# Attention value steps one unit further behind their scores, traced ahead of the scores of the unit that takes their buffer

## The chip, the core and the metric

The kernel runs on one core of one Trainium2 chip. The core has five engines that run side by side, each through its own list of instructions in order: TensorE (PE, matrix products; PEld is its weight load), VectorE (DVE), ScalarE (ACT), GpSimd (POOL) and SyncE (SP). SP computes nothing here: nearly all DMA transfers are issued from its queue, one behind the other. The metric is the device time of one execution in microseconds (us), lower is better.

## What is computed

Two layers of a decoder on 1024 tokens of width 1024. Layer 0 uses mixer A (dilated sliding-window attention), layer 1 mixer B (sliding-window attention with sinks). Each is followed by a layer norm and a gate. Cut to what matters:

```python
def mixer_a(x, w_in, w_out, cos, sin):
    h = x @ w_in
    for gi, (window, dil) in enumerate(((128, 1), (512, 4), (2048, 16))):
        q, k, v = ...                       # 16 heads of 64, rope on q and k
        o, lse = banded_attention(strided(q), strided(k), strided(v), window // dil)
        ...
    wts = softmax(stack(lses))              # the three groups are merged
    o = einsum('gbsh,gbshd->bshd', wts, stack(outs))
    return (o * silu(z)) @ w_out

def banded_attention(q, k, v, max_dist, sinks=None):
    s = einsum(q, k) * dh ** -0.5           # scores in a band of keys
    e = exp(s - max(s))
    return einsum(e, v) / sum(e), lse

x = layer_norm(ALPHA * x + h); x = x + sigmoid(x @ w_gate) * (p @ w_proj)
```

## The kernel before

**Linear work.** Products in full precision are made of three half-precision ones: each operand is split into a high and a low part, and `lin` (L264 on) issues L270, L271 and L272 for each of 8 slices of the contraction. So one tile of 128 tokens by 512 columns is 24 matmuls, called linear matmuls below. Mixer A has 6 times a block of `v` tiles and two blocks of `q`/`k` tiles (8 tiles each), then `z` tiles; mixer B has fewer. Weights come in blocks: loaded (L102), their largest value found (L108 on DVE), split (L131 on ACT, L132 on DVE) while earlier blocks are multiplied.

**Units.** The attention is cut into units of four heads and one tile of 128 queries, against one or two tiles of keys: 96 units in mixer A, 32 in mixer B, numbered from 0. A unit has two steps. `score` computes the scores on PE (L383, 8 or 16 matmuls into `s`), adds the mask and takes the maximum (L387, DVE), makes the bias `nbias` (L391, ACT, written into the unit's `st`), the exponentials (L393, ACT), splits them into `phl` (L397 ACT, L399 POOL or DVE), and has the DMA transpose `phl` into `pT` (L402, SP). `value` multiplies `pT` with the values (L414 to L416, 12 or 24 matmuls into one half of `o`), copies the result into `st` (L694, ACT) and stores `st` to a scratch in DRAM (L703, SP). In mixer B the result goes through `mu` (L858, DVE) instead. The units of a `q`/`k` tile start about 1.67 tiles after it, since `rope_out` has to rotate, split and transpose the tile into `qk` (L345 to L360).

**Order around the change.** `sub_tick` is called after every third of a linear tile and adds `upt` thirds of credit; a full credit calls `unit_step`. This takes the next unit from the queue, pushes it into `self.pipe`, a list of `lag` entries, and takes the oldest one out. So the value step of a unit is traced `lag` unit steps after its scores: 2 in mixer A, 3 in mixer B. `upt` is 0.75 in most of mixer A, so units come every 1.33 tiles. The tracing order is not the last word: the program is then put in order for each engine by a scheduler that goes by a timeline of its own, and may put an instruction behind later ones when its operands come late there.

**Buffers.** A tile name with `bufs=n` has n buffers that are taken in turn; whoever takes one waits for the last reader of its previous content. `pT` has `lag + 1` (3 in mixer A, 4 in mixer B), the scratch row `st` of mixer A `lag + 2` = 4. So the scores of unit u + 4 write the `st` that unit u stored.

**Merges.** When the last of three groups of a token tile has its value, `merge` (L745 to L767) loads the three `st` rows back as `gt`, weighs and adds them (DVE, POOL) and stores the sum to `oa`. In `mixed`, behind mixer A, these rows are loaded (L894), multiplied with the gate, split, transposed and multiplied with the output weights.

Of the kernel before, what the change touches and what calls it, by code (L numbers as in the profile page):

```python
# [10 lines left out]
F32 = mybir.dt.float32  # L11
F16 = mybir.dt.float16
# [8 lines left out]
P = 128  # L21
# [5 lines left out]
HD = 64  # L27
# [111 lines left out]
class Trunk:  # L139
# [160 lines left out]
    def unit_step(self):  # L300

        if not (self.units or any(self.pipe)):
            return
        new = self.units.pop(0) if self.units else None
        old = self.pipe.pop()
        self.pipe.insert(0, new)
        if new:
            new["score"]()
        if old:
            old["value"]()  # L310

    def set_lag(self, lag):
        assert not any(self.pipe)
# [56 lines left out]
    def scores(self, qa, kas, mask, cs, ncs, sums, nbias, floor, pool_lo):  # L370

        nc, at = self.nc, self.att
        nb = len(kas)
        nk = nb * P
        sm = at.tile([P, 4, 2 * P], F32, tag="sm", name="sm", bufs=self.bufs)
        mx = self.small.tile([P, 4], F32, tag="mx", name="mx", bufs=6)
        for pr in range(2):
            ps = self.ps_s.tile([P, 2, 2 * P], F32, tag="s", name="s")
            for i in range(2):
                h = 2 * pr + i  # L380
                for kb, ka in enumerate(kas):
                    for sw in range(2):
                        nc.tensor.matmul(ps[:, i, kb * P:(kb + 1) * P], qa(h), ka(h, sw), start=(sw == 0),  # L383
                                         stop=(sw == 1))
            for i in range(2):
                h = 2 * pr + i
                nc.vector.tensor_tensor_reduce(sm[:, h, :nk], ps[:, i, :nk], mask, 1.0, -3e38, ALU.add, ALU.max,  # L387
                                               mx[:, h:h + 1])
        if floor is not None:
            nc.vector.tensor_max(mx, mx, floor)  # L390
        nc.scalar.activation(nbias, mx, AF.Copy, scale=ncs, bias=LN_PSCALE)  # L391
        for h in range(4):
            nc.scalar.activation(sm[:, h, :nk], sm[:, h, :nk], AF.Exp, bias=nbias[:, h:h + 1], scale=cs,  # L393
                                 accum_out=sums[:, h:h + 1])
        pf = at.tile([P, 16 * P], F16, tag="phl", name="phl", bufs=self.bufs)
        hl = pf[:, :8 * nk].rearrange("p (a h c) -> p a h c", a=2, h=4)
        nc.scalar.activation(hl[:, 0], sm[:, :, :nk], AF.Copy)  # L397
        eng = nc.gpsimd if pool_lo else nc.vector
        eng.tensor_sub(hl[:, 1], sm[:, :, :nk], hl[:, 0])  # L399
        pt = at.tile([P, 2, 4, 2, P], F16, tag="pT", name="pT", bufs=len(self.pipe) + 1)  # L400
        ptf = pt.rearrange("p a h b c -> p (a h b) c")[:, :8 * nb, :]
        nc.sync.dma_start(ptf, pf[:, :8 * nk], transpose=True)  # L402
        return ptf.rearrange("p (a h b) c -> p a h b c", a=2, h=4)
# [218 lines left out]
    def layer_a(self):  # L622
        nc, tc, a = self.nc, self.tc, self.a
        at = self.att
        self.o_dr = [self.dram.tile([P, D], F32, name=f"oa{n}", tag=f"oa{n}") for n in range(NT)]
        self.z_dr = [self.dram.tile([P, D], F32, name=f"za{n}", tag=f"za{n}") for n in range(NT)]
        scr = [[self.dram.tile([S, 2, 4 * HD + 8], F32, name=f"scr{g}_{i}", tag=f"scr{g}_{i}") for g in range(3)]
               for i in range(2)]

        self.x2_scale()  # L630
        self.set_lag(2)
        self.upt = 0.75
        vh = at.tile([P, 3, NT, 4 * HD], F16, tag="vh", name="vh", bufs=1)
        vl = at.tile([P, 3, NT, 4 * HD], F16, tag="vl", name="vl", bufs=1)
        slots = [2, 2]
        cvs = {}
        for pair in range(2):
            for g in (1, 2, 0):
                self.rope_tables(g)
                blk = self.next_block()  # L640
                cvs[pair, g] = self.prod(self.invx, blk.inv, 2.0 ** V_SHIFT, "cv")
                slots = [i for i in range(3) if i != slots[1]]
                pick = slice(slots[0], slots[1] + 1, slots[1] - slots[0])
                for n in range(NT):
                    ps = self.ps_lin.tile([P, 512], F32, tag="lin", name="lin")
                    self.lin(ps, blk, *self.stat_a(g, n), 0, 512)
                    self.v_out(ps.rearrange("p (s c) -> p s c", s=2), vh[:, pick, n, :], vl[:, pick, n, :])
                    self.progress()
                blk.released = True
                for i in range(2):  # L650
                    if pair and g == 0 and i:
                        self.upt = 1.0
                    blk = self.next_block()
                    cs, ncs = self.qk_scales(blk, self.invx)
                    v1, v2 = (v[:, slots[i]].rearrange("p n (h c) -> p n h c", c=HD) for v in (vh, vl))
                    qk = []
                    for n in range(NT):
                        ps = self.ps_lin.tile([P, 512], F32, tag="lin", name="lin")
                        self.lin(ps, blk, *self.stat_a(g, n), 0, 512)
                        qk.append(at.tile([P, 12, P], F16, tag="qk", name="qk", bufs=8))  # L660
                        self.rope_out(ps, 4, 4, n, qk[n])
                        self.unit_a(2 * pair + i, g, n, qk, v1, v2, cs, ncs,
                                    cvs[pair, g], scr)
                        self.progress()
                    blk.released = True
        self.merge_every = 1
        self.z_block(self.invx, lambda n: self.stat_a(0, n))
        self.drain()
# [15 lines left out]
    def unit_a(self, q, g, n, qk, vh, vl, cs, ncs, cv, scr):  # L684
        nc, at = self.nc, self.att
        tiles = [n] if g == 2 or (n % 2 == 0 if g == 1 else n == 0) else [n - 1, n]
        mask = self.mask_2 if g == 2 else self.mask_a[:, (2 - len(tiles)) * P:]

        def stats():
            st = at.tile([P, 4 * HD + 8], F32, tag="st", name="st", bufs=len(self.pipe) + 2)  # L690
            return st, st[:, 4 * HD:4 * HD + 4], st[:, 4 * HD + 4:]

        def outp(o, st):
            nc.scalar.activation(st[:, 0:4 * HD], o.rearrange("p h c -> p (h c)"), AF.Copy, scale=cv)  # L694
            d = scr[q // 2][g][:, q % 2, :]
            if g == 1:
                b = 512 * (n % 2) + n // 2
                d = d[b:b + 509:4]
            elif g == 2:
                d = d[n:n + 1017:8]  # L700
            else:
                d = d[n * P:(n + 1) * P]
            nc.sync.dma_start(d, st)  # L703
            if g == 0 and q % 2:
                self.merges.append(self.merge(n, q // 2, scr[q // 2]))

        kas = [lambda h, sw, t=qk[i]: t[:, 4 + 4 * sw + h, :] for i in tiles]
        self.later(UNIT_LAG, lambda: self.unit(lambda h: qk[n][:, h, :], kas, mask, cs, ncs,
                                          lambda h, kb: vh[:, tiles[kb], h, :], lambda h, kb: vl[:, tiles[kb], h, :],
                                          stats, outp, n % 4 != 0))  # L710
# [76 lines left out]
    def layer_b(self, xT, invx):  # L787
        nc, at = self.nc, self.att
        self.o_dr = [self.dram.tile([P, D], F32, name=f"ob{n}", tag=f"ob{n}") for n in range(NT)]
        self.z_dr = [self.dram.tile([P, D], F32, name=f"zb{n}", tag=f"zb{n}") for n in range(NT)]  # L790
        self.set_lag(3)
        self.bufs = 3
        self.rope_tables(0)
        self.sk_cs = self.kv.tile([P, 16], F32, name="sk_cs", tag="sk_cs")
# [349 lines left out]
```

## Time and profile before

| | us |
|---|---|
| median of 3 runs (lowest) | 1680.08 (1678.07) |
| the profiled execution, its own time | 1672.76 |
| its span, first to last instruction | 1670.9 |
| PE busy | 1587.2 |
| DVE busy | 1080.0 |
| ACT busy | 922.0 |
| POOL busy | 671.6 |

The profile is one execution. Mixer A lies between 80 and 1000 us of its span, the output and gate of layer 0 up to 1250, mixer B from 1250 to 1480, the rest is output and gate of layer 1. A row of a waits view says which instruction of which engine stood idle, and whose end it was released by, with the sum, the number of times and the longest. A row of a timeline has the start, the length, the engine, line and operation, what it writes and reads, and, in brackets, the idle time before it. In a row of SP's queue the length is the time the issue of that transfer held the queue, not the transfer itself.

### The profile page before, as it was taken

Reading aid. Unit: us, or ns where it says so; the run is one execution under the profiler, and the core shown is the slowest. Engines: PE = TensorE matmul, PEld = TensorE weight load, DVE = VectorE, ACT = ScalarE, POOL = GpSimd, SP = SyncE. Lnnn points to the kernel's source line nnn. Section 1 sums busy time; section 2 is a strip of 40 time slices with the busy share of each in tenths; the row PEclk is TensorE's granted clock in tenths of the full one; section 3 lists DMA queues with packets and bytes.
Section 4 is the critical chain, followed back from the end, with each engine's and each line's share of the span. In section 5 each row is a group of like instructions: output and inputs, shape, how many; then the busy total and the mean of one; then the engine's idle time right before and its main releaser. Section 6 shows DMA issues by size and latency. Waiting matters only on the chain.

```text
span 1670.9 us, 29003 instructions
## 1 busy us (share of the span) xinstructions
PE 1587.2 (95%) x10579; PEld 879.7 (53%) x10579; DVE 1080.0 (65%) x2617; ACT 922.0 (55%) x2050; POOL 671.6 (40%) x481
## 2 busy tenths in 40 slices
PE   9899999999999889999999997789999999999999
PEld 3455666654555446666545543334456555544444
DVE  6756655655656875456556567788437989777731
ACT  4536755674775377556647844433333888854221
POOL 0205623532554665144235743343323452225441
PEclk9999999999999999999999998899999999999999
DMA  9617765774788777467648885989976798988963
GB/s 364 244 60 171 169 146 133 165 162 112 164 163 208 208 161 160 120 153 158 153 117 176 181 248 192 314 233 237 247 190 138 143 209 176 189 300 218 256 199 111
DMA packets 543791, 311.02 MB, mean 186 GB/s; under 512 B 473120, under 2 KB 494240, under 8 KB 543392
## 3 DMA queue, kind: packets, MB, share of 16 engines
q1 hardware_dynamic: 543648, 309.16, 73.6%
q8 instruction: 83, 1.36, 0.4%
q14 instruction: 60, 0.49, 0.1%
HBM read 137.78 MB, written 54.92 MB: 115 GB/s over the span
## 4 chain that ended last, share of the span: by engine, by line
PE 59%; DVE 14%; DMA 12%; issue 5%; POOL 4%; ACT 3%; SPq 2%; POOLq 0%; DVEq 0%; ACTq 0%
PE lin L270 18%; PE lin L272 18%; PE lin L271 18%; DMA pT<-phl 4%; DVE whl L132 3%; PE s L383 3%; DVE wpm L108 2%; DMA gt<-scr 2%; ACT sm L393 1%; DVE sm L387 1%; PE o L414 1%; PE o L416 1%; PE o L415 1%; POOL hl L356 1%; DMA wraw<-in_wg_dram 1%
## 5 line engine op out<-in xcount | busy, mean ns | idle before, releaser
L270 PE MATMUL lin<-whl,xhl 128*128 128x512 f16 x1280 | 488.9, 382 | 0.0
L271 PE MATMUL lin<-whl,xhl 128*128 128x512 f16 x1280 | 487.7, 381 | 0.0
L272 PE MATMUL lin<-whl,xhl 128*128 128x512 f16 x1280 | 487.5, 381 | 0.0
L399 POOL TENSOR_TENSOR phl<-sm,phl 128x1024 f16<-128x1024 f32 (+1 forms) x88 | 156.5, 1778 | 259.6 <-ACT phl L397 215.7
L349 POOL TENSOR_TENSOR t<-t,t 128x512 f32<-128x512 f32 (+1 forms) x120 | 152.2, 1268 | 232.1 <-DVE t L348 226.1
L272 PEld LDWEIGHTS <-xhl 128*128 128x128 f16 x1280 | 149.3, 117 | 125.8 <-issue 2.9
L270 PEld LDWEIGHTS <-xhl 128*128 128x128 f16 x1280 | 149.2, 117 | 117.4 <-issue 2.6
L108 DVE TENSOR_REDUCE wpm<-wraw 128x1 f32<-128x1024 f32 (+1 forms) x132 | 157.2, 1198 | 82.7 <-DMA wraw<-in_wa_dram 47.4
L271 PEld LDWEIGHTS <-xhl 128*128 128x128 f16 x1280 | 149.9, 117 | 115.2 <-issue 2.3
L393 ACT ACTIVATE sm<-sm,st,cs 128x128 f32<-128x128 f32 (+1 forms) x384 | 203.4, 531 | 3.3 <-ACT st L391 0.4
L356 POOL TENSOR_TENSOR hl<-t,hl 128x512 f16<-128x512 f32 (+1 forms) x120 | 142.7, 1189 | 136.0 <-ACT hl L355 136.0
L387 DVE CUSTOM_DVE_ANT_0 sm<-s,tab 128x256 f32<-128x256 f32 (+1 forms) x512 | 157.0, 359 | 53.7 <-PE s L383 51.9
L132 DVE SCALAR_TENSOR_TENSOR whl<-wraw,s,whl 128x1024 f16<-128x1024 f32 (+1 forms) x116 | 165.0, 1473 | 4.7 <-ACT whl L131 4.6
L345 DVE TENSOR_TENSOR t<-lin,rope 128x512 f32<-128x512 f32 (+1 forms) x120 | 78.9, 658 | 119.3 <-PE lin L272 83.1
L355 ACT ACTIVATE hl<-t 128x512 f16<-128x512 f32 (+1 forms) x120 | 72.1, 601 | 121.0 <-POOL t L349 119.2
L131 ACT ACTIVATE whl<-wraw,s 128x1024 f16<-128x1024 f32 (+1 forms) x116 | 121.9, 1122 | 12.6 <-DVE s L210 6.5
L272 PE MATMUL lin<-whl,x2T 128*128 128x512 f16 (+1 forms) x320 | 115.0, 359 | 0.0
L271 PE MATMUL lin<-whl,x2T 128*128 128x512 f16 (+1 forms) x320 | 115.0, 359 | 0.0
L270 PE MATMUL lin<-whl,x2T 128*128 128x512 f16 (+1 forms) x320 | 114.9, 359 | 0.0
L397 ACT ACTIVATE phl<-sm 128x1024 f16<-128x1024 f32 (+1 forms) x128 | 110.2, 861 | 2.7 <-DMA pT<-phl 1.5
L359 ACT ACTIVATE hl<-hl 128x512 f16<-128x512 f16 (+1 forms) x104 | 63.1, 607 | 59.0 <-POOL hl L356 58.8
L414 PEld LDWEIGHTS <-pT 128*128 128x128 f16 x800 | 72.2, 98 | 34.9 <-DMA pT<-phl 31.1
(190 smaller groups left out, 2901.7 us busy)
## 6 DMA issues: line engine op xcount, KB each, us to landing
wraw<-in_wa_dram SPq DMA_DIRECT2D x56, 512.0 KB, 5.2
scr<-st SPq DMA_DIRECT2D x96, 132.0 KB, 2.4
gt<-scr SPq DMA_DIRECT2D x48, 264.0 KB, 3.3
wraw<-in_wav_dram SPq DMA_DIRECT2D x24, 512.0 KB, 6.1
prh<-pro SPq DMA_DIRECT2D x32, 256.0 KB, 4.5
wraw<-in_wg_dram SPq DMA_DIRECT2D x16, 512.0 KB, 9.0
xg<-y SPq DMA_DIRECT2D x16, 512.0 KB, 3.7
wraw<-in_wb_dram SPq DMA_DIRECT2D x16, 512.0 KB, 6.3
```

The costliest lines, as they stand in the source:

```text
L108: k.nc.vector.tensor_reduce(pm[:, c:c + 1], self.raw[:, c * q:(c + 1) * q], axis=AX.X, op=ALU.max, apply_absolute_value=True)
L131: nc.scalar.activation(hl[:, 0, sl], self.raw[:, sl], AF.Copy, scale=self.s)
L132: nc.vector.scalar_tensor_tensor(hl[:, 1, sl], self.raw[:, sl], self.s, hl[:, 0, sl], op0=ALU.mult, op1=ALU.subtract)
L270: mm(ps, xh(kt), wh, start=(kt == 0), stop=False)
L271: mm(ps, xh(kt), wl, start=False, stop=False)
L272: mm(ps, xl(kt), wh, start=False, stop=(kt == NK - 1))
L349: nc.gpsimd.tensor_add(t1[:, :nh * HD], t1[:, :nh * HD], t2[:, :nh * HD])
L356: nc.gpsimd.tensor_sub(hl[:, :nh, HD:P], rv, hl[:, :nh, 0:HD])
L387: nc.vector.tensor_tensor_reduce(sm[:, h, :nk], ps[:, i, :nk], mask, 1.0, -3e38, ALU.add, ALU.max, mx[:, h:h + 1])
L393: nc.scalar.activation(sm[:, h, :nk], sm[:, h, :nk], AF.Exp, bias=nbias[:, h:h + 1], scale=cs, accum_out=sums[:, h:h + 1])
L397: nc.scalar.activation(hl[:, 0], sm[:, :, :nk], AF.Copy)
L399: eng.tensor_sub(hl[:, 1], sm[:, :, :nk], hl[:, 0])
```

## The change

In `unit_step` the value step of the oldest unit is now traced ahead of the scores of the new one. The lag is 3 in mixer A and 4 in mixer B. Since the value is traced first, its buffer of `pT` is free for the new unit, and the counts become `lag` for `pT` and `lag + 1` for `st`: 3 and 4 in mixer A, 4 in mixer B for `pT`, the same numbers as before.

```diff
@@ unit_step
         old = self.pipe.pop()
         self.pipe.insert(0, new)
+        if old:
+            old["value"]()
         if new:
             new["score"]()
-        if old:
-            old["value"]()
@@ scores
-        pt = at.tile([P, 2, 4, 2, P], F16, tag="pT", name="pT", bufs=len(self.pipe) + 1)
+        pt = at.tile([P, 2, 4, 2, P], F16, tag="pT", name="pT", bufs=len(self.pipe))
@@ layer_a
-        self.set_lag(2)
+        self.set_lag(3)
@@ unit_a, stats
-            st = at.tile([P, 4 * HD + 8], F32, tag="st", name="st", bufs=len(self.pipe) + 2)
+            st = at.tile([P, 4 * HD + 8], F32, tag="st", name="st", bufs=len(self.pipe) + 1)
@@ layer_b
-        self.set_lag(3)
+        self.set_lag(4)
```

On PE, the value step of unit 52, in mixer A. `lin` is a linear tile, `s_6963` are scores of unit 54, `s_7048` of unit 55, `pT_6767` is unit 52's. Before, it stands four linear matmuls behind the scores of unit 54 (one row of each kind is shown where rows repeat):

```order
L383 MATMUL s_6963<-qk_6691 128x128
L270 LDWEIGHTS xhl_106
L270 MATMUL lin_6934<-whl_6228,xhl_106 128x512
...
L414 LDWEIGHTS pT_6767
L414 MATMUL o_78<-vh_648,pT_6767 128x64
...
L271 MATMUL lin_6934<-whl_6228,xhl_106 128x512
...
L270 MATMUL lin_7013<-whl_6228,xhl_106 128x512
...
L383 MATMUL s_7048<-qk_6691,qk_6735 128x128
```

Now the rest of that tile and all 24 matmuls of the next one come first, and the value stands directly ahead of the scores of unit 55:

```order
L383 MATMUL s_6963<-qk_6665 128x128
...
L270 MATMUL lin_6999<-whl_6181,xhl_106 128x512
...
L272 MATMUL lin_6999<-whl_6181,xhl_106 128x512
L414 LDWEIGHTS pT_6767
L414 MATMUL o_78<-vh_648,pT_6767 128x64
...
L383 LDWEIGHTS qk_6709
L383 MATMUL s_7048<-qk_6665,qk_6709 128x128
```

26 more linear matmuls lie ahead of it. The scores of unit 55 were followed by the value of unit 53; now the value of unit 52 precedes them.

In SP's queue, at the same place: `pT_6767`, `pT_6876`, `pT_6978` are the transposes of units 52 to 54, `st_6742` is the stored row of unit 52, `wraw` a weight load, `qk` the transposes of later `q`/`k` tiles. Before:

```order
L402 DMA_TRANSPOSE pT_6767<-phl_6764 128x8x128
L360 DMA_TRANSPOSE qk_6819<-hl_6825 128x12x128
L703 DMA scr1_1_621<-st_6624 128x264
L102 DMA wraw_7110<-in_wa_dram 128x1024
L402 DMA_TRANSPOSE pT_6876<-phl_6873 128x16x128
L703 DMA scr1_1_621<-st_6742 128x264
L360 DMA_TRANSPOSE qk_6919<-hl_6925 128x12x128
L402 DMA_TRANSPOSE pT_6978<-phl_6975 128x8x128
```

Now:

```order
L402 DMA_TRANSPOSE pT_6767<-phl_6764 128x8x128
L360 DMA_TRANSPOSE qk_6805<-hl_6811 128x12x128
L703 DMA scr1_1_621<-st_6527 128x264
L102 DMA wraw_7084<-in_wa_dram 128x1024
L402 DMA_TRANSPOSE pT_6876<-phl_6873 128x16x128
L703 DMA scr1_1_621<-st_6624 128x264
L360 DMA_TRANSPOSE qk_6893<-hl_6899 128x12x128
L402 DMA_TRANSPOSE pT_6978<-phl_6975 128x8x128
L703 DMA scr1_1_621<-st_6742 128x264
```

The store of unit 52 has moved from behind the transpose of unit 53 to behind that of unit 54. The transposes themselves and the weight load keep their places. From the output rows of layer 0 on, through mixer B to the end, the instructions on PE, DVE, ACT and POOL stand in the same order in both programs.

## Rows read from the trace of the kernel before

**Rows 1.** The page, part 1: busy us, share of the span, instructions.
```profile
PE 1587.2 (95%) x10579; PEld 879.7 (53%) x10579; DVE 1080.0 (65%) x2617; ACT 922.0 (55%) x2050; POOL 671.6 (40%) x481
```

**Rows 2.** PE's waits, 0 to 1000 us: us in total, times, longest.
```profile
PE o L414 <- DMA pT<-phl: 18.6, 14, 2.8
PE s L383 <- DMA qk<-hl: 6.6, 4, 2.1
```

**Rows 3.** PE's waits, 500 to 570 us.
```profile
PE o L414 <- DMA pT<-phl: 6.5, 5, 2.3
PE o L414 <- ACT sm L393: 0.7, 1, 0.7
```

**Rows 4.** PE's waits, 570 to 600 us.
```profile
PE s L383 <- DMA qk<-hl: 4.8, 3, 2.1
PE o L414 <- DMA pT<-phl: 0.7, 1, 0.7
```

**Rows 5.** PE's waits, 900 to 1000 us.
```profile
PE o L414 <- DMA pT<-phl: 2.6, 3, 1.1
PE s L383 <- DMA qk<-hl: 1.8, 1, 1.8
```

**Rows 6.** Timeline of PE: start us, us, instruction, [idle before <- releaser].
```profile
300.21 0.38 PE L270 MATMUL lin<-whl,xhl 128*128 128x512 f16 x1
300.42 0.38 PE L271 MATMUL lin<-whl,xhl 128*128 128x512 f16 x1
...
605.66 0.61 PE L383 MATMUL s<-qk 128*128 128x128 f16 x8
...
626.50 0.20 PE L414 MATMUL o<-vh,pT 128*128 128x64 f16 x1 [2.73 <-DMA pT<-phl]
```

**Rows 7.** PE's waits, 1000 to 1150 us.
```profile
PE s L235 <- DVE mdd L228: 8.8, 1, 8.8
```

**Rows 8.** PE's waits in mixer B, 1250 to 1480 us.
```profile
PE o L414 <- DMA pT<-phl: 4.8, 3, 2.5
```

**Rows 9.** Stretch; PE, PEld, DVE, ACT, POOL busy (count); granted clock; DMA share; GB/s.
```profile
200.00:250.00 50.00, 47.21 (x358) 32.06 (x357) 26.51 (x71) 31.75 (x82) 15.27 (x9) 0.97 0.61 143
...
500.00:550.00 50.00, 44.88 (x390) 26.92 (x388) 32.26 (x99) 25.10 (x70) 23.98 (x17) 1.00 0.82 207
550.00:600.00 50.00, 42.42 (x254) 22.57 (x253) 41.11 (x89) 23.87 (x56) 34.91 (x27) 0.97 0.74 189
```

**Rows 10.** Timeline of SP's DMA queue, at the unit of rows 6.
```profile
619.17 4.41 SPq L402 DMA_TRANSPOSE pT<-phl  x1
```

**Rows 11.** Timeline of POOL and DVE, 944 to 957 us.
```profile
944.60 1.28 POOL L349 TENSOR_TENSOR t<-t,t 128x512 f32<-128x512 f32 x1
...
953.15 3.99 DVE L132 SCALAR_TENSOR_TENSOR whl<-wraw,s,whl 128x1024 f16<-128x1024 f32 x2
...
953.81 2.24 POOL L349 TENSOR_TENSOR t<-t,t 128x512 f32<-128x512 f32 x1
```

**Rows 12.** What the DMA queue of SP waited for, whole span.
```profile
SPq L102 <- DVE whl L132: 69.5, 22, 22.1
```

**Rows 13.** Timeline of PE, ACT and SP, 450 to 465 us.
```profile
450.26 0.19 PE L414 MATMUL o<-vh,pT 128*128 128x64 f16 x1
...
453.09 7.74 SPq L402 DMA_TRANSPOSE pT<-phl  x1
...
458.08 1.06 PE L383 MATMUL s<-qk 128*128 128x128 f16 x16
...
461.72 0.30 ACT L391 ACTIVATE st<-mx,ncs 128x4 f32<-128x4 f32 x1 [0.62 <-DVE mx L387]
...
464.59 0.57 SPq L703 DMA_DIRECT2D scr<-st  x1
```

**Rows 14.** L391, what ACT waited for (us, times); L703, time to landing.
```profile
  DMA scr<-st: 3.0, 2
...
DMA to landing us min/median/max: 1.7/2.4/6.2
```

## The prediction

> **What bounds the kernel now.** I read the page's first part first: PE is busy 95% of the span, the next engine, DVE, 65% [rows 1]. A time is gained here only where PE stands still, or where its clock is down. So I next asked for PE's own waits by stretch. In mixer A (up to 1000 us) the value matmuls of L414 wait for the transposed weights `pT` 14 times, 18.6 us in all, and the score matmuls of L383 for `qk` 6.6 us [rows 2]. The waits of L414 fall into three kinds. Five stand in 500 to 570, with a sixth that another releaser is named for: 6.5 + 0.7 us; behind them, in 570 to 600, `qk` takes 4.8 us and `pT` 0.7 us [rows 3, 4]. Three stand at the tail, 900 to 1000: 2.6 us, with 1.8 us for `qk` [rows 5]. What is left of the 14 are 5 lone waits: 18.6 - 6.5 - 0.7 - 2.6 = 8.8 us; the longest is 2.8 us [rows 2], another 2.73 us [rows 6]. From 1000 to 1150 PE waits for weights and output rows, not for any unit [rows 7]. In mixer B, L414 waits 4.8 us for `pT` [rows 8].
>
> A wait costs more than its idle figure. Matmuls of 512 columns start 0.22 us apart but are drawn 0.38 us long [rows 6], so each gap hides another 0.16 us. And the mean granted clock, 1.00 in 500 to 550, is 0.97 in 200 to 250, where the longest lone wait stands, and in 550 to 600, behind the dense waits [rows 9]: 0.03 x 50 = 1.5 us each.
>
> **What the change moves.** No operation is added or removed; only the order is other. On PE the value matmuls of mixer A lie further behind their scores. For units 6 to 83 it is 10 to 42 more linear matmuls in the program order, mostly 30 to 33, at 0.22 us each: some 7 us. The unit in the first order fence has its scores at 605.66 and its value at 626.50, after 2.73 us of waiting [rows 6]; its transpose was issued at 619.17 and held the queue 4.41 us [rows 10]. In the changed order 26 more linear matmuls lie ahead of that value: 26 x 0.22 = 5.7 us against 2.73 us late. So this wait goes.
>
> The sum, term by term:
>
> (a) Lone waits. They are at most 2.8 us, and their units move by 16 to 26 matmuls, 3.5 to 5.7 us, so all five are covered: 8.8 + 5 x 0.16 + 1.5 for the clock at 225 = 11.1 us gained. The stretches around them are PE-bound, so what is gained stays gained. Lower bound, if the longest wait stays with its clock: 11.1 - 2.8 - 0.2 - 1.5 = 6.6.
>
> (b) The dense stretch, 500 to 600. The waits on `pT` hold 6.5 + 0.7 + 0.7 + 7 x 0.16 + 1.5 = 10.5 us. Here the chain behind the scores is slow for several units in a row, since the merges of finished rows share SP's queue, DVE and POOL with it. More distance absorbs a delay once, about 7 us, and not again for each unit. PE then reaches the `qk` waits of 4.8 us earlier and may wait longer there. DVE is busy 32.3 and 41.1 us in the two halves [rows 9], with some 27 us of 100 to spare, so the chain can follow in part. Bounds: 0 (all given back at `qk`) and 10.5 + 4.8 = 15.3. I take half of the `pT` part, 5.
>
> A rule speaks against (b). In 953 to 958 two L132 take 3.99 us, 2.0 each, and L349 on POOL beside them 2.24 us, where it took 1.28 alone [rows 11]. The Trainium skill, "SBUF — State Buffer", section "Summary: rules for kernel authors", says that when a DVE operation has two SBUF inputs while a GpSimd operation reads SBUF, the one that issues second is held until the first is through. By that rule the busy figures of DVE and POOL in this stretch hold waiting for each other, the chain has no room, and (b) would be 0 and the sum 10. The trace shows both slower and not which of them was held.
>
> (c) The tail. In the changed order the last scores of mixer A stand 20 linear matmuls earlier, and the last four value steps 9 to 20 earlier, up to 4.4 us. PE may therefore wait up to 4.4 us more than the 2.6 + 1.8 us of today. But after it PE waits 8.8 us for weight maxima anyway [rows 7], which swallow it; gone, that cover would cost the 4.4 us. I take 0, bounds +4.4 gained and 4.4 lost.
>
> (d) Mixer B. Its value steps are traced one step later too, but PE's, DVE's, ACT's and POOL's rows stand in the same order in both programs: the scheduler already puts each value behind the scores of a later unit. The ring of `pT` has 4 buffers as before. So the 4.8 us stay: 0, bounds 0 and 4.8 gained.
>
> (e) A new wait. `st` keeps 4 buffers, but its owner now holds one for a unit longer. Before, the store of unit u had until the scores of u+4, two units after its value. Now it has one: 33 linear matmuls, 7.3 us, and about 1.5 us for the value and one group of scores, 8.8 in all; L391 comes 3.6 us behind its scores (458.08 and 461.72 [rows 13]), so 12.4 us are allowed. In SP's queue the store now stands behind the transpose of a later unit (second order fence), and SP waits 69.5 us for weight splits over the run, 22.1 us at the longest [rows 12]. One of the two longest cases: value at 450.26, store at 464.59, after a transpose that holds SP for 7.74 us [rows 13], then 0.6 us of issue and 2.4 us to landing [rows 14]: 17.3 us after the value, 4.9 too late. ACT waits so far only twice, 3.0 us [rows 14]. Paired over the trace, 12 of the 96 stores are issued more than 9 us behind their value; at some 2 us for each that is 24 us of ACT waiting. Behind L391 in ACT's queue stand the exponentials, L355 and L359 of the next `qk`, and the `vh` copies that free PSUM. What covers it is the new distance: for the unit of the first fence scores to value is now 626.50 - 605.66 - 2.73 + 5.7 = 23.8 us of PE work, and its slow chain needed 20.8, so 3.0 us are spare, and more for quicker units. I take 1 us lost; bounds 0 and 24.
>
> The sum: 11.1 + 5 + 0 + 0 - 1 = 15 us. The profiled execution took 1672.76 us (span 1670.9); the median of the runs shown is 1680.08, 7.3 above it. So 1657.8 on the profile's own time and 1665 as a median.
>
> **The rivals.**
>
> The forecast: lone waits gone, dense stretch half gone, gain 8 to 24 us, 1656 to 1672. For it: every lone wait is shorter than its unit's move. Chance 0.60.
>
> R1, the wait moves to `qk` and the merges: (b) is 0 and (a) at its lower bound, the gain 6.6 - 1 = 5.6 us, 1674; anything from 0 to 8 counts here. For it: `qk` waits already follow directly on the `pT` waits [rows 4]. Against: DVE's spare share. The rule of the Trainium skill on DVE and GpSimd, named above, speaks for this rival too. Chance 0.22.
>
> R2, the `st` ring becomes the bound: ACT waits for stores, and its delay reaches PE through `qk` and the next `pT`. If all 24 us came through, the time is 1680 - 16 + 24 = 1688. It decides once an ACT wait exceeds what its unit has spare, 3.0 us for a slow one. For it: SP is one queue, and the case shown is already 4.9 us late. Against: 84 of the 96 stores come in time, and a late store and a late chain need not meet in one unit. Chance 0.11.
>
> R3, all waits on `pT` go, the `qk` ones with them, and the tail too: 11.1 + 15.3 + 4.4 = 30.8, 1649. It needs DVE and SP to follow PE at once. Chance 0.07.
>
> That the change does nothing is true of mixer B, and is in the sum; for mixer A the order on PE shows the move in nearly every unit.
>
> **How the numbers follow.** 1665 is the likeliest case; 8 times in 10 the time should lie between 1651 and 1682: that leaves out the far end of R3 and most of R2. The likeliest case alone gives 1656 to 1672. Two per cent, about what a measurement of this kernel can tell from no change, is 33.6 us: faster than 1646.5 needs more than R3's whole sum (0.06); slower than 1713.7 needs R2 with twice its price (0.03); within it 0.91.
>
> **What would show it.** Right: PE's waits of L414 for `pT` up to 900 fall from 16 us to under 4; clock 1.00 in 200 to 250; the L414 waits in mixer B as before; a new row of ACT L391 waiting for the DMA `scr<-st` with 5 to 25 us, and no PE wait behind it. (b) is wrong if the `qk` waits of L383 grow above 10 us; (e) if PE waits for `pT` at units behind such an ACT wait; (c) if the stretch 1000 to 1150 gets longer.

## The result and the profile after

The changed kernel takes 1665.19 us against 1679.07 us for the kernel before, each the median of four runs. One run of each (2053.30 and 3079.18 us) was in a slow state and counts in no ratio; the middle of the other three is 1662.87 and 1678.07. The ratio, by which all runs here are compared, is 0.9932, with a 95% interval of 0.9909 to 0.9955: 11.4 us less, between 7.6 and 15.3. The prediction was 1665 us, between 1651 and 1682. The two profiled executions lie only 5.2 us apart (1672.76 and 1667.52, spans 1670.9 and 1665.7): before's lies below its timed runs (1676.91 is their lowest), after's above the lowest two of its own (1662.28, 1662.87). So the sizes below are read from rows, and the total from the ratio.

The page of after, part 1, which answers to [rows 1]:

```profile
PE 1592.0 (96%) x10579; PEld 883.1 (53%) x10579; DVE 1085.1 (65%) x2617; ACT 923.8 (55%) x2050; POOL 677.8 (41%) x481
```

The work is the same; PE's idle time fell from 1670.9 - 1587.2 = 83.7 to 1665.7 - 1592.0 = 73.7 us. The span fell by 5.2 us only, since PE was also busy 4.8 us longer with the same 10579 matmuls. Where the idle time fell is read from a table by stage (PE's busy time is the first figure after the length of the stretch, the granted clock the third from the end). First the kernel before:

```profile
200.00:300.00 100.00, 97.21 (x666) 66.19 (x665) 53.70 (x144) 61.62 (x155) 35.99 (x26) 0.98 0.59 138
300.00:500.00 200.00, 199.27 (x1427) 113.02 (x1426) 119.88 (x325) 132.64 (x328) 89.58 (x68) 1.00 0.70 153
500.00:600.00 100.00, 87.30 (x643) 49.49 (x641) 73.37 (x187) 48.97 (x125) 58.89 (x43) 0.98 0.78 198
600.00:900.00 300.00, 294.75 (x2077) 180.97 (x2076) 172.18 (x472) 192.44 (x478) 122.29 (x94) 1.00 0.63 145
900.00:1150.00 250.00, 217.53 (x1356) 106.14 (x1355) 183.33 (x408) 126.46 (x243) 120.62 (x77) 0.95 0.85 231
1250.00:1500.00 250.00, 234.60 (x2130) 139.04 (x2128) 203.06 (x570) 179.40 (x439) 89.05 (x70) 0.99 0.85 193
```

Then the changed kernel:

```profile
200.00:300.00 100.00, 97.55 (x688) 66.91 (x686) 54.30 (x145) 61.90 (x155) 37.86 (x27) 0.98 0.63 140
300.00:500.00 200.00, 200.00 (x1451) 113.91 (x1448) 123.10 (x325) 133.52 (x329) 89.85 (x66) 1.00 0.71 153
500.00:600.00 100.00, 86.35 (x614) 49.35 (x613) 76.51 (x183) 48.22 (x122) 60.13 (x42) 0.93 0.73 191
600.00:900.00 300.00, 298.78 (x2112) 183.68 (x2111) 179.59 (x483) 196.91 (x489) 129.02 (x96) 1.00 0.67 149
900.00:1150.00 250.00, 223.31 (x1364) 108.37 (x1363) 177.72 (x411) 125.62 (x235) 120.05 (x77) 0.95 0.91 239
1250.00:1500.00 250.00, 233.42 (x2077) 134.63 (x2076) 203.61 (x568) 177.97 (x433) 88.36 (x67) 0.98 0.86 190
```

PE gained 0.3 + 0.7 us in 200 to 500, 4.0 in 600 to 900 and 5.8 in 900 to 1150. It lost 1.0 in 500 to 600, where the clock went from 0.98 to 0.93, and 1.2 in mixer B. So the dense stretch, which was to give 5 us, gave nothing, and the end of mixer A, put at 0, gave the most.

The windows are fixed in time and hold slightly different work in the two executions. Counted instead by equal work (the columns that PE has multiplied so far, from the same two traces), the changed execution is 2.5 us ahead where before stands at 500 us, 0.9 behind at 600, 3.7 ahead at 900, 1.7 behind at 1020, 7.7 ahead at 1250 and 5.2 ahead at the end. The kernel with mixer B as before (`x2_b_as_before`, below), which has the whole change in mixer A, is 4.3, 4.1, 7.6, 3.1, 13.7 and 10.4 us ahead at these places. Both say the same of the stages: a gain outside the dense stretch, none in it, a loss at the last units, and a larger gain in the output rows behind them. The dense stretch cost the changed execution 3.4 us and the other one 0.1.

PE's waits of after, 0 to 1000 us, beside [rows 2]:

```profile
PE s L383 <- DMA qk<-hl: 9.9, 6, 4.0
PE o L414 <- ACT st L694: 8.7, 4, 4.9
PE o L414 <- DMA pT<-phl: 5.7, 3, 4.7
```

The waits for `pT` fell from 18.6 us in 14 to 5.7 us in 3. 5.5 us of what is left stand at the tail, which had 2.6 [rows 5]:

```profile
PE o L414 <- DMA pT<-phl: 5.5, 2, 4.7
PE s L383 <- DMA qk<-hl: 1.6, 2, 1.0
```

So up to 900 us 0.2 us remain of 16. Unit 52, which before waited 2.73 us at 626.50 [rows 6], now starts its value at once. In the timeline of PE it is the first row, and the scores of unit 55 follow directly:

```profile
622.51 0.19 PE L414 MATMUL o<-vh,pT 128*128 128x64 f16 x1
...
623.21 0.61 PE L383 MATMUL s<-qk 128*128 128x128 f16 x8
```

But two new rows have come. One is a wait for `qk` where PE had none in that stretch before, here in the timeline:

```profile
268.57 0.62 PE L383 MATMUL s<-qk 128*128 128x128 f16 x8 [2.45 <-DMA qk<-hl]
```

The other, 8.7 us for `ACT st L694`, stands wholly in 500 to 570, where the five `pT` waits of [rows 3] were. With it, in 570 to 600, stands `PE s L383 <- DMA qk<-hl: 4.9, 2, 4.0` where [rows 4] had 4.8 us. The timeline of PE shows three of the four waits:

```profile
534.23 0.19 PE L414 MATMUL o<-vh,pT 128*128 128x64 f16 x1 [2.54 <-ACT st L694]
...
543.53 0.19 PE L414 MATMUL o<-vh,pT 128*128 128x64 f16 x1 [1.02 <-ACT st L694]
...
557.96 0.21 PE L414 MATMUL o<-vh,pT 128*128 128x64 f16 x1 [4.93 <-ACT st L694]
```

`pT` is there by now; what is missing is the copy L694 of the unit directly before. It doesn't matter here that this unit has the other half of `o`. The value step ahead of the one at 534.23 ran at 522.81. The copy before that, of the unit that had the same half as the one at 534.23, was over at 520.06; yet PE waited until the next copy was over, at 534.18:

```profile
519.59 0.47 ACT L694 ACTIVATE st<-o,cv 128x256 f32<-128x256 f32 x1
...
522.81 0.19 PE L414 MATMUL o<-vh,pT 128*128 128x64 f16 x1
```

In none of the 96 units of mixer A, before or after, does a value step start before the copy of the unit directly before has ended. So the two halves don't work as two buffers; why not is not shown. ACT takes its list in order, and its own timeline at these places is:

```profile
533.60 0.22 ACT L752 ACTIVATE mw<-mw 128x24 f32<-128x24 f32 x1 [3.80 <-DVE mw L751]
533.73 0.46 ACT L694 ACTIVATE st<-o,cv 128x256 f32<-128x256 f32 x1
...
542.90 0.22 ACT L752 ACTIVATE mw<-mw 128x24 f32<-128x24 f32 x1 [3.16 <-DVE mw L751]
543.03 0.46 ACT L694 ACTIVATE st<-o,cv 128x256 f32<-128x256 f32 x1
...
553.30 4.25 ACT L131 ACTIVATE whl<-wraw,s 128x1024 f16<-128x1024 f32 x4
557.45 0.46 ACT L694 ACTIVATE st<-o,cv 128x256 f32<-128x256 f32 x1
```

L694 stands behind the exponential of a merge, L752, which waits 3.8 and 3.2 us for the merge's step on DVE, and once behind four weight splits of 4.25 us.

In 1000 to 1150 us, beside [rows 7]:

```profile
PE s L235 <- DVE mdd L228: 13.6, 2, 7.4
PE lin L270 <- DMA ogT<-rhl: 4.6, 3, 2.9
```

The 13.6 us for weight maxima are two waits. The one of before, 8.75 us at 1036.16, is now 6.17 at 1035.32. The other, 7.44 us at 1061.33, stands where before had a wait that [rows 7] does not show, `PE lin L270 <- ACT whl L131: 10.2, 1, 10.2`, at 1064.86. So this wait has another releaser now and is 2.8 us shorter. The waits for output rows between 1110 and 1150 fell from 9.1 to 5.6 us; one of those of before is 4.4 us for L924.

### The profile page after: what moved, and what is told of

The parts are those of the page before. It is cut to its first block, busy times and chain, and to the rows that moved or that the text cites. A ratio compares the mean times of both kernels' runs of the same rounds, so it can differ in the third digit from the quotient of the medians.

```text
span 1665.7 us, 29033 instructions
## 1 busy us (share of the span) xinstructions
PE 1592.0 (96%) x10579; PEld 883.1 (53%) x10579; DVE 1085.1 (65%) x2617; ACT 923.8 (55%) x2050; POOL 677.8 (41%) x481
## 5 line engine op out<-in xcount | busy, mean ns | idle before, releaser
L270 PE MATMUL lin<-whl,xhl 128*128 128x512 f16 x1280 | 489.9, 383 | 0.0
L399 POOL TENSOR_TENSOR phl<-sm,phl 128x1024 f16<-128x1024 f32 (+1 forms) x88 | 155.1, 1763 | 234.6 <-ACT phl L397 213.0
L270 PEld LDWEIGHTS <-xhl 128*128 128x128 f16 x1280 | 149.5, 117 | 120.0 <-issue 4.3
L132 DVE SCALAR_TENSOR_TENSOR whl<-wraw,s,whl 128x1024 f16<-128x1024 f32 (+1 forms) x116 | 169.2, 1510 | 9.6 <-ACT whl L131 9.5
L131 ACT ACTIVATE whl<-wraw,s 128x1024 f16<-128x1024 f32 (+1 forms) x116 | 121.8, 1123 | 7.0 <-DVE s L210 7.0
L270 PE MATMUL lin<-whl,x2T 128*128 128x512 f16 (+1 forms) x320 | 114.9, 359 | 0.0
L383 PE MATMUL s<-qk 128*128 128x128 f16 x1120 | 81.8, 221 | 9.9 <-DMA qk<-hl 9.9
```

The source lines that it names most:

```text
L131: nc.scalar.activation(hl[:, 0, sl], self.raw[:, sl], AF.Copy, scale=self.s)
L132: nc.vector.scalar_tensor_tensor(hl[:, 1, sl], self.raw[:, sl], self.s, hl[:, 0, sl], op0=ALU.mult, op1=ALU.subtract)
L270: mm(ps, xh(kt), wh, start=(kt == 0), stop=False)
```

## The experiments

### Order or distance

The swap alone, on the kernel before:

```diff
         self.pipe.insert(0, new)
+        if old:
+            old["value"]()
         if new:
             new["score"]()
-        if old:
-            old["value"]()
```

> The kernel before with the two steps of unit_step swapped and nothing else: lag 2 and 3, pT and st with the buffers of before. If the gain comes from the distance (the lag), the swap alone shortens the way from scores to value by one group of scores, some 0.5 to 1 us for each unit: the waits of PE L414 for pT grow from 18.6 us up to 1000 us to 22 to 30, and the time is that of before or up to 12 us above it (1679 to 1692). If the gain came from the order (value ahead of scores), most of the 11 us should show here too: 1665 to 1670.

Measured: 1678.71 against 1674.83 us, ratio 1.0025 [1.0013, 1.0038]. PE's waits, 0 to 1000:

```profile
PE o L414 <- DMA pT<-phl: 17.6, 14, 4.3
```

The waits for `pT` stay where they were, 17.6 us against 18.6, and don't grow to the 22 to 30 expected. The swap by itself gives nothing and costs 4 us. This kernel and the changed one differ in the lag alone, so the gain is that of the distance: (1.0025 - 0.9932) x 1679 = 16 us. The swap only lets the distance grow with the same number of buffers.

The changed kernel with mixer B as before:

```diff
-        pt = at.tile([P, 2, 4, 2, P], F16, tag="pT", name="pT", bufs=len(self.pipe))
+        pt = at.tile([P, 2, 4, 2, P], F16, tag="pT", name="pT", bufs=self.pt_bufs)
@@ layer_b
-        self.set_lag(4)
+        self.set_lag(3)
```

(`pt_bufs` is 3 in mixer A, 4 in mixer B.)

> The changed kernel with mixer B's lag left at 3 (its pT ring stays at 4 buffers). PE, DVE, ACT and POOL have the same order as in the changed kernel, SP's queue differs in 7 places. If the longer lag does nothing in mixer B, the time is that of the changed kernel within 4 us (1661 to 1669), with the same PE waits in 1250 to 1480 (about 9 us for mu, 3 for pT). If the longer lag in mixer B matters, it differs by more: 1 to 5 us faster if the 4 us that PE lost more there in the changed profile came from it.

Measured: 1663.54 us, ratio 0.993 [0.9918, 0.9943], the same as with the whole change. Mixer B's part of the change does nothing.

### What bounds the dense stretch

The merges of the first pair of head groups, cut to one load and one store, on the changed kernel (`x5_merge_light`) and on the kernel before (`x5b_merge_light_before`). Their output is not the merged row.

```diff
-        for g in range(3):
+        for g in range(1 if pair == 0 else 3):
             nc.sync.dma_start(gt[:, g], scr[g][n * P:(n + 1) * P])
         sums, nb = gt[:, :, :, 4 * HD:4 * HD + 4], gt[:, :, :, 4 * HD + 4:]
         yield
+        if pair == 0:
+            nc.sync.dma_start(self.o_dr[n][:, pair * 512:(pair + 1) * 512].rearrange("p (a c) -> p a c", a=2),
+                              gt[:, 0, :, 0:4 * HD])
+            return
```

> The changed kernel with the merges of the first pair left out but for one load and one store each (no weighing, no loads of the other two groups); that part of the computation is missing, some 24 us of DVE, 30 us of POOL and 16 loads in 500 to 600 us. If the merges are what holds the dense stretch back (ACT's copy L694 behind the merge's exponential L752 in ACT's queue, the gt loads in SP's), PE's idle time in 500 to 600 falls from 13.6 us to under 4 and the clock there stays at 1.00: 12 to 18 us less than the changed kernel, 1647 to 1653. If the split of the next weight block on ACT and DVE is what holds it, more than 8 us of idle time stay, and the time falls by less than 6.

> The kernel before with the merges of the first pair left out but for one load and one store each, as in the run x5_merge_light of the changed kernel, which took 1647.3 us; the same part of the computation is missing. If the merges bound the dense stretch in both kernels, PE's loss in 500 to 600 goes here too (idle from 12.7 us to under 4), and what is left between the two is the lone waits, term (a): 8 to 12 us, so 1655 to 1660. If instead the pT waits in the dense stretch come from the short distance itself, they stay, and the two differ by 15 us or more: 1662 to 1668.

Measured: 1647.31 us, ratio 0.9838 [0.9821, 0.9855], on the changed kernel; 1661.81 us, ratio 0.9915 [0.9901, 0.9928], on the kernel before. The stretch in the light form of the changed kernel, where `PE s L383 <- DMA qk<-hl: 1.3, 1, 1.3` is the only wait of PE that is left:

```profile
500.00:600.00 100.00, 98.68 (x747) 58.08 (x746) 57.44 (x152) 62.17 (x148) 38.58 (x26) 1.00 0.78 189
```

Without the merges the stretch is as good as full, at full clock, in both orders (97.45 us busy in the light form of before). In the light form of before, L414 waits for `pT` up to 1000 us fell from 18.6 us in 14 to 9.5 in 8: the `pT` waits of the dense stretch came from the merges and not from the distance itself. The merges cost the kernel before 0.0085 x 1679 = 14 us, and the changed one (0.9932 - 0.9838) x 1679 = 16 us: the change has not relieved them. Beside light merges it is worth 0.9838/0.9915 = 0.992, some 13 us (8 to 12 expected), which comes from outside the dense stretch.

Which part of a merge is it? First the wait that the trace points at. The exponential of these merges is taken off ACT, so that L694 has no L752 ahead of it; the weights of these merges are then not those of the reference:

```diff
-        nc.scalar.activation(w, w, AF.Exp)
+        if pair == 0:
+            nc.vector.tensor_scalar(w, w, 1.0, None, op0=ALU.mult)
+        else:
+            nc.scalar.activation(w, w, AF.Exp)
```

> The changed kernel; in the eight merges of the first pair of head groups the exponential L752 on ACT is replaced by a small DVE copy of the same 24 columns (so these weights aren't the reference's); loads, products and the store of a merge stay, and the order on PE is the same but for nothing. Theory A (in the dense stretch the value matmuls wait because L694 on ACT stands behind L752, which waits for the merge's load): the waits of the value matmuls for L694 in 500 to 570, 8.7 us in the changed kernel, fall under 2; the time PE loses in 500 to 600 falls by 7 to 10 us, and the ratio to the kernel before goes from 0.993 to 0.987 to 0.989. Theory B (the merges' loads and products on SP, DVE and POOL set the pace; L694 is only where it shows): the L694 waits fall, but pT, qk or another releaser takes their place in the same stretch, and the ratio stays 0.991 to 0.995. For the lone waits elsewhere neither expects anything.

Measured: ratio 0.9944 [0.9928, 0.996]. PE's waits, 500 to 600, and the stretch:

```profile
PE s L383 <- DMA qk<-hl: 5.8, 2, 3.9
PE o L414 <- ACT st L694: 5.7, 2, 4.0
```

```profile
500.00:600.00 100.00, 87.93 (x626) 50.36 (x625) 74.42 (x197) 47.83 (x116) 61.26 (x42) 0.95 0.76 196
```

The waits for L694 fell by 3.0 us, not by 7; PE gained 1.6 us there and the time nothing. Its longest, 4.0, now ends behind the four L131 alone:

```profile
549.99 4.25 ACT L131 ACTIVATE whl<-wraw,s 128x1024 f16<-128x1024 f32 x4
554.14 0.46 ACT L694 ACTIVATE st<-o,cv 128x256 f32<-128x256 f32 x1
```

So the exponential that stands ahead of L694 is not what the time hangs on: theory B of this run holds. The 5.7 us of waits that are left say nothing either way on L694 behind L131. The next run keeps the three loads and the store of these merges, and leaves out all work between them (the loop over the loads stays as it was, the early `return` above is kept):

> The changed kernel; the merges of the first pair of head groups keep their three loads (L745) and their store, and leave out all work between: the reductions, the exponential and the products on DVE, ACT and POOL (their output is then not the merged row). It parts the two halves of what the light merges (one load, one store, ratio 0.9838) had left out. If the work on DVE, ACT and POOL sets the pace of the dense stretch: as with the light merges, ratio 0.982 to 0.986, PE busy over 97 of 100 us in 500 to 600. If the loads in SP's queue set it: ratio 0.991 to 0.995, PE busy under 90 of 100 us there, with waits for pT or qk. In between, each has a share, read from the same rows.

Measured: 1656.55 us, ratio 0.988 [0.9858, 0.9901]. The stretch, where PE waits only for `qk`, 5.3 us in two waits:

```profile
500.00:600.00 100.00, 94.70 (x688) 54.71 (x687) 50.28 (x139) 56.67 (x134) 34.19 (x23) 0.95 0.82 210
```

In between: of the 16 us, (0.9932 - 0.988) x 1679 = 9 belong to the work on DVE, ACT and POOL, and (0.988 - 0.9838) x 1679 = 7 to the two further loads, each give or take 5 by the intervals. Neither part of the merge is the whole of it. With the work gone L694 makes PE wait no more, and what PE then waits for is `qk`.

Two more tried to free this stretch otherwise. One yield more between a merge's loads and its first step on DVE, `yield` set behind the first one:

> The changed kernel; each merge pauses for one tile more between its loads and its first DVE operation (one more yield behind the loads). On ACT the exponential of a merge still stands ahead of the L694 of the dense stretch in most places. Theory A (L752 waits for the merge's load): the load gets a tile's time, 5 us, more, so the wait of ACT for L751 and with it the L694 waits shrink where the order has moved, up to 5 us gained. Theory B: the merges' work is the same, the waits only move: within 2 us of the changed kernel, ratio 0.991 to 0.995.

Measured: 1665.51 us, ratio 0.9946 [0.9925, 0.9966]; `PE o L414 <- ACT st L694: 8.3, 4, 4.9` in 500 to 570. More time for the load moves nothing: theory B again.

Four places for `o` instead of two, with a fourth buffer of `s` given up for the space, and a control with the three buffers of `s` alone:

```diff
-        self.ps_s = ec(tc.tile_pool(name="ps_s", bufs=4, space=PSUM))
+        self.ps_s = ec(tc.tile_pool(name="ps_s", bufs=3, space=PSUM))
@@ only in x14_o4
-        self.o_ps = self.ps_o.tile([P, 2, 4, HD], F32, tag="o", name="o")
+        self.o_ps = self.ps_o.tile([P, 4, 4, HD], F32, tag="o", name="o")
-        self.o_i ^= 1
+        self.o_i = (self.o_i + 1) % 4
```

> The changed kernel with four places for o in PSUM in place of two; the bank for it is taken from the scores (three buffers of s in place of four). The scheduled order is that of x15_s3. If the wait of PE L414 for ACT L694 in 500 to 570 (8.7 us) costs what it shows, it goes, and the time is 5 to 10 us below x15_s3. If the merges set the pace of the stretch, that wait turns into one for qk or pT and the time is that of x15_s3 within 3 us.

> The changed kernel with three buffers of s in place of four and nothing else: what x14_o4 is compared with. All theories: the waits of L414 for L694 in 500 to 570 stay at 8 to 10 us; the time is that of the changed kernel or up to 8 us above it, where scores wait for the DVE to free a buffer (1663 to 1672).

Measured: 1680.33 us, ratio 1.0032 [1.002, 1.0044], and 1681.25 us, 1.0033 [1.002, 1.0045]. Over the run the wait for L694 stands at 7.6 us with four places and at 7.7 without: it did not go away. With four places too a value step waits for the copy of the unit directly before (one starts at 541.15, 0.05 us after that copy), so this pair doesn't show what a free place in `o` would be worth. Places that are tiles of their own were not tried. What the pair shows is the price of the fourth `s`: (1.0033 - 0.9932) x 1679 = 17 us, against up to 8 expected.

### The ring of `st`

The stores L703 issued from ACT's own queue instead of SP's, on the changed kernel:

```diff
-            nc.sync.dma_start(d, st)
+            nc.scalar.dma_start(d, st)
```

> The changed kernel with the stores of st (L703) issued from ACT's queue right behind the copy L694, instead of from SP's. If the place in SP's queue is what makes the store late, ACT's waits for scr<-st fall from 20.7 us to under 3. If these waits cost PE nothing, as the prediction's term (e) has it, the time changes by that alone by less than 3 us; what comes on top is that gt loads start earlier and SP's queue is 96 issues shorter (a gain of 2 to 8 us in 500 to 600 and at the tail), less 96 issues on ACT. If the st ring costs PE more than assumed, 5 to 15 us are gained.

In the changed kernel ACT waits for the old store, as predicted (L391, what ACT waited for):

```profile
  DMA scr<-st: 20.7, 7
```

With the stores in ACT's queue:

```profile
  DMA scr<-st: 4.3, 2
```

Measured: 1664.42 us, ratio 0.9937 [0.9925, 0.995]. 16 us of waiting on ACT have gone and the time is the same; the 2 to 8 us that SP's shorter queue was to give on top didn't come. The waits of PE for L694 stay at 9.4 us in 500 to 570, so these aren't the ring's doing either.

### One unit further still

Lag 4 in mixer A, with 4 buffers of `pT` and 5 of `st`, and its control. Both give up a buffer of the rope table and one of `hl` for the space:

```diff
-        t = self.const.tile([P, N_ROPE], F32, name="rope", tag="rope", bufs=2)
+        t = self.const.tile([P, N_ROPE], F32, name="rope", tag="rope", bufs=1)
-        hl = w.tile([P, 12, P], F16, tag="hl", name="hl", bufs=3)
+        hl = w.tile([P, 12, P], F16, tag="hl", name="hl", bufs=2)
@@ only in x9_lag4
-        self.set_lag(3)
+        self.set_lag(4)
```

> The changed kernel with one buffer of the rope table instead of two and two of hl instead of three, lag 3: the control of the run with lag 4. If these buffers have slack, it is within 2 us of the changed kernel (ratio 0.992 to 0.995); if hl was needed, the qk waits of L383 grow by several us and the time with them.

> The changed kernel with one unit more of distance in mixer A: lag 4, so four buffers of pT and five of st; the space comes from one buffer instead of two for the rope table and two instead of three for hl. Its control is the next run, with these two cuts and lag 3. Theory (the lone waits are gone already at lag 3 and the dense stretch is paced by the merges): within 3 us of the control; pT waits up to 900 stay under 1 us. Rival (distance was still short in the dense stretch): 500 to 600 loses 5 us or more less, and the time is 5 to 10 us below the control.

Measured: the control 1665.04 us, ratio 0.9937 [0.9922, 0.9952], as the changed kernel; lag 4 1679.55 us, 1.0022 [1.0012, 1.0033]. All of the gain is gone, which neither theory expected. The control by stage:

```profile
500.00:600.00 100.00, 87.42 (x623) 50.16 (x621) 77.38 (x186) 47.97 (x122) 62.72 (x44) 0.95 0.74 198
...
900.00:1150.00 250.00, 220.14 (x1336) 106.89 (x1334) 176.39 (x407) 122.64 (x227) 118.52 (x76) 0.95 0.91 240
```

With lag 4:

```profile
500.00:600.00 100.00, 87.47 (x635) 50.45 (x633) 69.39 (x178) 46.10 (x118) 55.85 (x40) 0.95 0.78 184
...
900.00:1150.00 250.00, 206.63 (x1275) 99.89 (x1274) 174.32 (x390) 116.96 (x221) 115.51 (x74) 0.92 0.84 224
```

Early on PE is full (100.00 us busy in 200 to 300, against 97.71 in the control). The dense stretch is the same (87.47 and 87.42 us), as the theory on the merges wants. The loss is behind mixer A, 13.5 us of PE's time, and most of it in one place. The timeline of PE with lag 4:

```profile
1065.52 0.59 PE L270 MATMUL lin<-whl,ogT 128*128 128x512 f16 x1 [19.52 <-issue]
```

PE has no linear work left and waits for the first output row; in the control 8.84 + 0.27 us are lost there. Three later waits for output rows hold 9.8 us with lag 4 and 6.2 in the control. The chain to the first row starts with the load of the merged rows (L894), and SP issues it behind the last merge's store (L767). In SP's queue of the control:

```profile
1012.91 1.27 SPq L745 DMA_DIRECT2D gt<-scr  x3
...
1030.80 0.37 SPq L767 DMA_DIRECT2D oa<-gt  x1
```

and with lag 4:

```profile
1026.40 1.27 SPq L745 DMA_DIRECT2D gt<-scr  x3
...
1037.85 0.37 SPq L767 DMA_DIRECT2D oa<-gt  x1
```

The last merge ends 7.05 us later, and the load of the merged rows comes 7.36 later (1041.33 against 1033.97). Its values are not late: the last value step starts at 986.10 with lag 4 and at 986.64 in the control. What is late are its own loads, by 13.5 us. In both kernels no merge is stored for 17 to 19 us, while DVE is busy with weight blocks as well (1007.47 to 1024.27 with lag 4, 1008.96 to 1027.75 in the control). With lag 4 three of the last eight merges are still to be stored then, in the control two, and the last one of lag 4 is loaded only behind this pause.

## Why the prediction was right, and where it was not

The median, 1665.19 us, is the predicted one, and the gain of 11.4 us lies inside the forecast's 8 to 24. But the sum came out by two terms that were off against each other.

**(a) Lone waits: right in kind, too large.** All five are gone, as the 0.2 us up to 900 show, and the clock in 200 to 250 is 1.00 (it was 0.97, [rows 9]):

```profile
200.00:250.00 50.00, 50.00 (x384) 35.18 (x382) 28.56 (x80) 35.76 (x92) 16.37 (x10) 1.00 0.63 146
```

But the next 50 us now hold the `qk` wait of 2.45 us, and a clock of 0.97. By the tables PE gained 1.0 + 4.0 = 5.0 us in 200 to 500 and 600 to 900, against 8.8 us of waits and 11.1 us in all that the term counted. The failed step is "the stretches around them are PE-bound, so what is gained stays gained": the value steps could be late no more, but the scores behind them then could. With lag 4 that wait is gone too (100.00 of 100 us in 200 to 300).

**(b) The dense stretch: wrong, nothing instead of 5.** The idle time on `pT` went, and the same stretch gave it back as 8.7 us for L694 beside 4.9 for `qk`: 100 - 86.35 = 13.7 us idle against 12.7 before. The failed step is "with some 27 us of 100 to spare, so the chain can follow in part". An engine's spare share over 100 us says little on a chain whose links wait for each other. A merge goes from DRAM through SP to DVE, ACT, POOL and back to SP, and each engine takes its list in order, so the copies and the transposes of the units stand behind its links. That much of this is argued from the lists; what the light merges show is the size: 16 us of the changed kernel hang on them, 14 of the kernel before. Rival R1 had the give-back, though with the wait at `qk`; it came mostly at `o`, a resource that no term had looked at. For that reason the sign that was to show (b) wrong did not quite appear: the `qk` waits came to 9.9 us, not above 10.

The Trainium skill's rule on DVE and GpSimd ("SBUF — State Buffer", section "Summary: rules for kernel authors") gave 0 for (b), which is what came. The trace of the changed kernel agrees, and shows what [rows 11] left open, which engine is held:

```profile
539.82 2.13 POOL L399 TENSOR_TENSOR phl<-sm,phl 128x1024 f16<-128x1024 f32 x1
...
539.86 2.64 DVE L766 TENSOR_TENSOR gt<-gt 128x512 f32<-128x512 f32 x1 [0.34 <-POOL gt L763]
...
548.03 0.69 DVE L766 TENSOR_TENSOR gt<-gt 128x512 f32<-128x512 f32 x1 [0.26 <-POOL gt L763]
```

With POOL idle, L766 of a merge takes 0.69 us. Started 0.04 us behind POOL's L399 it takes 2.64 and ends 0.55 us after L399: DVE was held. Behind it on DVE stands L751, for which ACT's L752 at 542.90 waits, and behind that the copy L694 and PE's 1.02 us at 543.53. The 2.54 us at 534.23 stand behind such a pair as well (L766 at 530.60, 2.60 us). It is a part of the chain and not all of it: with the DVE, ACT and POOL work of the merges gone, 5.3 us of idle time and a clock of 0.95 are left in the stretch, and about 7 of the 16 us come back only with the loads left out. What the holding alone costs was not tried.

**(c) The tail: a loss and a larger gain, put at 0.** As said, PE waits longer at the last units, 5.5 + 1.6 us against 2.6 + 1.8. The first wait for weight maxima behind them swallowed that, as forecast: it fell from 8.75 to 6.17 us. The failed step is "PE waits for weights and output rows, not for any unit": these rows come behind the last merge, and so behind the last units. The next wait fell from 10.23 to 7.44 us and those for output rows by 3.5, and PE's busy time in 900 to 1150 rose by 5.8 us, past the bound of 4.4. The chain ahead of these rows was earlier: the last merge was stored at 1033.92 instead of 1036.73, and the first matmul of an output row came at 1061.89 instead of 1064.86, though the last value step starts at nearly the same time (991.92 and 992.11). The wait for L131 stands in the two other kernels with the old distance as well (10.5 us in `x1_order_only`, 10.7 in `x5b_merge_light_before`), and in none of the runs with lag 3. So the shift goes with the distance; why the last merge ends earlier was not tried. With lag 4 it ends later, and 13.5 us are lost in this stretch.

**(d) Mixer B: right on the time.** It runs the same with its old lag: ratio 0.993 without that part, 0.9932 with it. Its waits moved all the same, since what it waits for is not fixed to one releaser. After, 1250 to 1480, beside [rows 8]:

```profile
PE o L414 <- DVE mu L858: 8.7, 6, 2.7
PE o L414 <- DMA pT<-phl: 2.8, 2, 1.8
```

The forecast "the waits as before" was too narrow there: 4.8 us for `pT` became 2.8, and the wait for `mu`, 5.2 us in before, became 8.7. With mixer B as before they are 2.7 and 7.6, and with the swap alone 2.6 and 8.5, so it isn't the lag of B that did it.

**(e) The ring of `st`: right.** 20.7 us of waiting on ACT lie within the 5 to 25 of the forecast, and no time hangs on them: taking 16 us of them away changed the ratio from 0.9932 to 0.9937. R2 is out.

**The sum.** Forecast 11.1 + 5 + 0 + 0 - 1 = 15; read by the stages 5.0 - 1.0 + 5.8 - 1.2 = 8.6 us of idle time, beside a clock that is lower in 500 to 600. That the ratio gave 11.4 and the median the very figure of the forecast is partly luck: (a) and (b) were too high by about 12, (c) too low by about 6. And the sum starts from the profiled execution of before, which lay below its timed runs: on that scale 1657.8 was forecast, and the profiled execution of the changed kernel took 1667.52.

No version was found that beats the changed kernel: mixer B as before, the stores on ACT, the later merges and the smaller buffers all came to 0.993 to 0.995.

## What to carry to other kernels

More distance between a producer and its consumer takes away single waits and does nothing for a stretch in which some other chain sets the pace; to find out which it is, make that other chain light in both versions and compare. Don't take the instruction that ends a wait last for its cause: look at what stands ahead of it in its engine's list, and take that away before believing it. Check that two buffers are two: see whether a producer ever starts before the copy of the result directly before has ended. And look at the end of the loop when the distance grows: one unit was worth 11 us and the next cost 14, as the last results came 7 us later to work that had no cover.

## What the runs showed that was not expected

- The granted clock doesn't follow from the idle time alone. With the same `qk` wait at 200 to 300 (97.55, 97.56 and 97.71 us busy) it was 0.98 in the changed kernel, and 1.00 with mixer B as before and with the smaller buffers. In 500 to 600 it was 0.93 in the changed kernel and 0.95 to 0.97 in its near copies. So the 1.5 us that term (a) took for a clock of 0.97 are no fixed price of such a wait.
- A buffer of scores in PSUM was worth more than the whole change: three `s` instead of four cost 17 us, and most of what it adds to PE's waits is not at the scores but at output rows, `PE lin L270 <- DMA ogT<-rhl: 27.7, 6, 10.7` over the run.
- Waits that look alike differ greatly in price: 16 us less on ACT for the stores gave nothing, and the merges, which showed up as 13.6 us of PE's waits, gave 16 us when they were made light.
